# Running sums of the gates as rows of a product, and the last two heads' mask on TensorE, in a hybrid decoder block

## Chip, cores and metric

The kernel runs on one core of a Trainium2 chip. The metric is the time of the whole program on the device, in microseconds, taken as the median of several runs; smaller is better. A core has five engines with queues of their own, worked off in order: TensorE (PE in the profile, its weight loads PEld), VectorE (DVE), ScalarE (ACT), GpSimd (POOL) and SyncE (SP, which here only starts DMAs). Matrix products are written to the accumulator memory PSUM; all other tiles lie in the on-chip memory SBUF, and larger intermediate arrays in device memory.

## The reference

A decoder block over 1024 tokens of width 1024: forgetting attention (8 heads of 64) and a chunked spatial gate side by side, an output projection, then a gated MLP with a causal depthwise convolution. The change concerns the attention:

```
xn = rmsnorm(h, norm_mix_g); proj = xn @ w_in
log_f = log_sigmoid(proj[..., G_END:] + b_forget)          # one gate per head and token
c = cumsum(log_f, axis=1)
logits = einsum('bqhd,bkhd->bhqk', q, k) * Dh ** -0.5
logits = logits + c_q - c_k                                # running sums of query and key
logits = where(causal, logits, -inf)
p = softmax(logits); out = einsum('bhqk,bkhd->bqhd', p, v)
mix = concat([out, spatial_gate], -1); h = h + mix @ w_out
```

In a softmax over the keys the query's own sum `c_q` cancels, so the kernel needs only the key's `c_k`.

## The kernel before

**Precision.** Operands of the large products are split into a high part, rounded to the type in which TensorE takes them, and a low part, the rest; a product is made of high x high, high x low and low x high.

**Stages.** Queries, keys, gates and values are projected first. Queries and keys go to device memory as `qd` and `kd` (head, high or low, 64, 1024), through stores on SP's queue (L534). `forget` and `forget_sums` make the gates' running sums; `turn` transposes them to rows of 64 x 128, negates them and stores them as `ncd` (8 x 1024), from the middle of the first query and key step. Behind the attention come the output projection (L1026 to L1028) and the gated MLP (L1117, L1369).

**Attention.** `head_loads(h)` brings a head's operands: `ab[:, 0]` holds the query's high and low part on 64 partitions each, `ab[:, 1]` the key's likewise, `b2s` the key's parts in swapped order, and `cks` the row of `ncd` repeated on all 128 partitions. The head's two small tiles alternate between even and odd heads. `logits(h, j)` makes the logits of query block j (128 rows) for its (j+1) x 128 keys: in pieces of up to 512 columns two products, `A x B` (high x high plus low x low) and `A x B2` (high x low plus low x high), into one of two buffers of two PSUM banks (tag `L`). The signs are turned, so that masked entries are large and a minimum is sought. On POOL, `affine_select` sets the entries above the diagonal of the block's own 128 columns of `cks` to 3e38. Since a later (larger) block reads these columns unmasked, and blocks run from 7 down to 0, each select stands between two minima. On DVE one fused instruction adds logits and row, writes the result to SBUF and gives the row minimum; ACT takes the exponential of it in place with its sum.

`turn_p` transposes blocks of exponentials on PE, ACT copies the high part and DVE subtracts the low part (L813 to L815); `values` multiplies them with V (L832) and `row_tail` turns the reciprocal row sums (L738 to L742). `pair_half` scales and splits the outputs of two heads, for the first three pairs on POOL.

**Order.** PE's order in the attention is written out by hand: `seq` chains every PE instruction behind the one before. A step holds two groups of value products of head h, the transposes of the next step, and, by the table `NEXT`, up to two query blocks of logits of head h+1. Heads 6 and 7's logits are made in the steps of heads 5 and 6. Sixteen pieces of filler (`sg_out`, L874 to L876, twelve products each: the projection of the spatial gate) are spread over the steps up to head 4's by `FILLS`; their weights come in two halves, and the second half's low parts are made on DVE (called from L880). On the other engines a scheduler decides the order when the program is built, by program order and readiness; `after` adds an order without a wait. The lists `sels` hold the selects, and behind them `pair_half` and `wo_load` (splitting the output weights) are ordered on POOL, one instruction behind each select.

Of the kernel before, what the change touches and what calls it, by code (L numbers as in the profile page):

```python
# [14 lines left out]
P = 128  # L15
# [50 lines left out]
def block_kernel(ctx: ExitStack, tc: tile.TileContext, xT, xtok, wuv, wv, wqk, wf, cpk, bfv,  # L66
# [73 lines left out]
    qd = drm.tile([8, 2, 64, 1024], F32, name="qd")  # L140
    kd = drm.tile([8, 2, 64, 1024], F32, name="kd")
    rbd = drm.tile([8, P], F32, name="rbd")
    ncd = drm.tile([8, 1024], F32, name="ncd")
    vd = drm.tile([2, P, 2, 512], F32, name="vd")
    hpd = drm.tile([8, P, 1024], F32, name="hpd")
    h2d = drm.tile([8, P, 1024], F32, name="h2d")
# [309 lines left out]
    def forget():  # L456

        c = sb("gg", [P, 512])
        r = sb("gg", [P, 512], F32R)
        wfa, sel = c[:, 0:128].rearrange("p (a b) -> p a b", b=8), c[0:64, 128:136]  # L460
        bfb, z, e, rows = c[:, 136:144], c[:, 144:208], c[:, 208:272], c[0:64, 272:400]
        tri, ones, lh, ll = r[:, 0:P], r[:, P:2 * P], r[:, 256:320], r[:, 320:384]
        sp.dma_start(out=wfa[:, 0:8, :], in_=wf)
        sp.dma_start(out=bfb, in_=bfv.to_broadcast((P, 8)))
        dve.tensor_tensor(out=wfa[:, 8:12, :], in0=wfa[:, 0:4, :], in1=wfa[:, 4:8, :], op=ALU.add)
        dve.tensor_scalar(out=wfa[:, 12:16, :], in0=wfa[:, 0:4, :], scalar1=-1.0, scalar2=None, op0=ALU.mult)
        dve.tensor_tensor(out=sel, in0=ident[0:64, 0:8], in1=ident[0:64, 32:40], op=ALU.add)

        one128 = one[:, 0:1].to_broadcast((P, P))
        act.copy(ones, one128)  # L470
        dve.scalar_tensor_tensor(out=tri, in0=maskb, scalar=0.0, in1=ident, op0=ALU.is_gt, op1=ALU.add)
        w = sb(RTAG[rn[0] % 6], [P, 16, 64], F32R)
        rn[0] += 1
        dve.memset(f32(w), 0.0)
        dve.tensor_copy(w[:, :, 0:8], wfa)
        dve.tensor_tensor(out=w[:, :, 32:40], in0=wfa, in1=f32(w[:, :, 0:8]), op=ALU.subtract)
        zr = sb(RTAG[rn[0] % 6], [64, 1024])
        rn[0] += 1
        for hf in range(2):
            ps = sbank()  # L480
            ops = ([("B11", k, k) for k in range(4)] + [("B21", k, 4 + k) for k in range(4)] if hf == 0 else
                   [("B22", k, 8 + k) for k in range(4)] + [("T3", k, 12 + k) for k in range(4)])
            for i, (n, k, wi) in enumerate(ops):
                for s in range(2):
                    pe.matmul(ps[0:64, :], w[:, wi, :], xs(n, s, k), start=(i == 0 and s == 0),
                              stop=(i == 7 and s == 1))
            act.copy(zr[:, hf * 512:hf * 512 + 512], ps[0:64, :])
        return c, r, zr

    def forget_sums(c, r, zr):  # L490
        sel, bfb, z, e, rows = c[0:64, 128:136], c[:, 136:144], c[:, 144:208], c[:, 208:272], c[0:64, 272:400]
        tri, ones, lh, ll = r[:, 0:P], r[:, P:2 * P], r[:, 256:320], r[:, 320:384]
        v3 = lambda t: t.rearrange("p (h t) -> p h t", h=8)
        ps = sbank()
        for tt in range(8):
            pe.matmul(ps[:, tt * 8:(tt + 1) * 8], zr[:, tt * P:(tt + 1) * P], sel, start=True, stop=True)
        dve.tensor_tensor(out=v3(z), in0=ps[:, 0:64].rearrange("p (t h) -> p h t", h=8),
                          in1=rstd1.unsqueeze(1).to_broadcast((P, 8, 8)), op=ALU.mult)
        dve.tensor_tensor(out=v3(z), in0=v3(z), in1=bfb.unsqueeze(2).to_broadcast((P, 8, 8)), op=ALU.add)
        dve.scalar_tensor_tensor(out=e, in0=z, scalar=-1.0, in1=z, op0=ALU.mult, op1=ALU.max)  # L500
        act.activation(e, e, AF.Exp, scale=-1.0)
        act.activation(e, e, AF.Ln, bias=one[:, 0:1])
        dve.tensor_scalar(out=z, in0=z, scalar1=-1.0, scalar2=0.0, op0=ALU.mult, op1=ALU.max)
        dve.tensor_tensor(out=z, in0=z, in1=e, op=ALU.add)
        dve.tensor_copy(lh, z)
        dve.tensor_tensor(out=ll, in0=z, in1=f32(lh), op=ALU.subtract)

        for o, m in ((64, tri), (128, ones)):
            pe.matmul(ps[:, o:o + 64], m, lh, start=True, stop=False)
            pe.matmul(ps[:, o:o + 64], m, ll, start=False, stop=True)  # L510
        whole, run = v3(ps[:, 128:192]), v3(e)
        dve.memset(run[:, :, 0:1], 0.0)
        for tt in range(1, 8):
            dve.tensor_tensor(out=run[:, :, tt:tt + 1], in0=run[:, :, tt - 1:tt], in1=whole[:, :, tt - 1:tt], op=ALU.add)
        dve.tensor_tensor(out=v3(z), in0=v3(ps[:, 64:128]), in1=run, op=ALU.add)

        def turn():
            pe.transpose(ps[0:64, 192:320], z, ident)
            act.activation(rows, ps[0:64, 192:320], AF.Copy, scale=-1.0)
            sp.dma_start(out=ncd.rearrange("h (t p) -> (h t) p", p=P), in_=rows)  # L520

        return turn

# [204 lines left out]
    loads = [None] * 8  # L728
    exs = []
    rows = [None] * 8  # L730
    sels = [[] for _ in range(8)]

    def row_tail(h):

        p, hh, rs = h // 2, h % 2, rows[h]
        ptr = bank()
        rt = sb("t01", [8, P])
        dve.reciprocal(rs, rs)  # L738
        seq(pe.transpose(ptr[0:8, 0:P], rs, ident))
        act.copy(rt, ptr[0:8, 0:P])  # L740
        act.dma_start(out=rsd[h], in_=rt)
        sp.dma_start(out=attF[p][hh * 64:hh * 64 + 64, 1, :],  # L742
                     in_=rsd[h].rearrange("a b -> (a b)").unsqueeze(0).to_broadcast((64, 1024)))

    def pair_half(p, o):

        if attT[p] is None:
            attT[p] = sb("A" if p < 2 else "G", [P, 2, 1024], F32R)
        f, t = attF[p], attT[p]
        if p < 3:  # L750
            s = sels[2 * p + 3][o.start // 512 * 3:]
            after(tc, pool.tensor_tensor(out=f[:, 0, o], in0=f[:, 0, o], in1=f[:, 1, o], op=ALU.mult), s[0])
            after(tc, pool.tensor_copy(t[:, 0, o], f[:, 0, o]), s[1])
            after(tc, pool.tensor_tensor(out=t[:, 1, o], in0=f[:, 0, o], in1=f32(t[:, 0, o]), op=ALU.subtract), s[2])
# [6 lines left out]
    psa.release()  # L761
    psa = tc.alloc_tile_pool(name="psb", bufs=4, space=bass.MemoryType.PSUM, reuse_waits="tile")

    cks, b2s = sb("x2", [P, 2, 1024]), sb("x2", [P, 2, 1024], F32R)
    abs_, places = [None] * 8, {}

    def head_loads(h):
# [1 line left out]
        abs_[h] = ab  # L769
        hh = h % 2  # L770
        sp.dma_start(out=f32(ab[:, 0, :]), in_=qd[h].rearrange("s d t -> (s d) t"))
        sp.dma_start(out=f32(ab[:, 1, :]), in_=kd[h].rearrange("s d t -> (s d) t"))
        sp.dma_start(out=cks[:, hh, :], in_=ncd[h:h + 1, :].to_broadcast((P, 1024)))
        sp.dma_start(out=f32(b2s[0:64, hh, :]), in_=kd[h, 1])
        loads[h] = sp.dma_start(out=f32(b2s[64:128, hh, :]), in_=kd[h, 0])
        rows[h] = sml.tile([P, 8], F32, tag="rs", name=nm("rs"))

    def logits(h, j):


        i, jj, hh = j // 2, j % 2, h % 2
        A, B, ck, B2 = abs_[h][:, 0, :], abs_[h][:, 1, :], cks[:, hh, :], b2s[:, hh, :]
        w1, w2 = (2 * i + 1) * P, (2 * i + 2) * P
        if jj == 1:
            tp = sb(TTAG[i][hh], [P, w1 + w2])
# [1 line left out]
        t = places[h, i][jj]  # L787
        n = (j + 1) * P
        qs = slice(j * P, (j + 1) * P)
        sels[h].append(pool.affine_select(out=ck[:, qs], in_=ck[:, qs], pattern=[[-1, P]], compare_op=ALU.is_ge,  # L790
                                          fill=BIG, base=0, channel_multiplier=1))
        mn = sml.tile([P, 1], F32, tag="mn", name=nm("mn"))
        ps = psa.tile([P, 1024], F32, tag="L", bufs=2, name=nm("pl"))
        for c in range(0, n, 512):
            e = min(n, c + 512)
            seq(pe.matmul(ps[:, c:e], A[:, qs], B[:, c:e], start=True, stop=False))  # L796
            seq(pe.matmul(ps[:, c:e], A[:, qs], B2[:, c:e], start=False, stop=True))  # L797
        dve.tensor_tensor_reduce(out=t, in0=ps[:, 0:n], in1=ck[:, 0:n], scale=1.0, scalar=lim[:, 0:1],  # L798
                                 op0=ALU.add, op1=ALU.min, accum_out=mn)
        exs.append(act.activation(t, t, AF.Exp, bias=mn, scale=-1.0, accum_out=rows[h][:, j:j + 1]))  # L800

# [43 lines left out]
    def sg_out():  # L845
# [17 lines left out]
        for hf in range(2):  # L863
            o = slice(hf * 512, hf * 512 + 512)
            for tt in range(8):
# [11 lines left out]
                dve.tensor_tensor(out=hs, in0=ps, in1=hs, op=ALU.add)  # L877
                sp.dma_start(out=hpd[tt, :, o], in_=hs)
                if hf == 0 and tt == 7:
                    whs = split(nxt, "dve")  # L880
                yield

    filler = sg_out()
# [3 lines left out]
    def wo_load(ks):  # L887
        for k in ks:
# [6 lines left out]
                w = [t[:, :, hf * 512:hf * 512 + 512] for hf in range(2)]  # L895
            for hf in range(2):
                src = wr[:, hf * 512:hf * 512 + 512]
                s = sels[6][4 * k + 2 * hf:] if k < 2 else sels[7][7:] * 2
                after(tc, pool.tensor_copy(w[hf][:, 0], src), s[0])
                after(tc, pool.tensor_tensor(out=w[hf][:, 1], in0=src, in1=f32(w[hf][:, 0]), op=ALU.subtract), s[1])  # L900
            wo.append(w)

    STEPS = [[(h, i, 2 * c) for i in (3, 2, 1, 0) for c in range(i + 1)] for h in range(8)]
# [612 lines left out]
```

## Time and profile before

| | |
|---|---|
| time, median of 3 runs | 1076.82 us (1076.59 to 1077.02) |
| the profiled execution | 1076.44 us, its span 1074.7 us |
| granted TensorE clock | 0.998 |
| PE busy | 1054.8 us, 98% of the span |
| DVE, ACT, POOL busy | 892.9, 571.0, 237.2 us |
| attention | about 222 to 387 us of the span |

A row of a view names the line of the kernel, the engine, the operation, the tile written and those read (buffer numbers left out), the shape and the count, then the busy time, the mean of one in ns, the idle time of the engine just before such instructions and what ended it. In a view by time a row begins with the start and the duration in microseconds. A wait is written as waiting engine and tile, arrow, the engine and tile that ended it, then total, count and longest wait. PE's matmuls overlap in their pipeline: one of 512 columns shows 389 ns, yet the next starts 227 ns later, so that short gaps between starts don't show as idle time.

### The profile page before, as it was taken

What the parts mean: (1) busy time and instruction counts of PE and PEld (TensorE: products, weight loads), DVE (VectorE), ACT (ScalarE), POOL (GpSimd) and SP (SyncE); (2) the same over time, 40 slices, a digit from 0 to 9 for tenths busy, and PEclk for the clock granted to TensorE, in tenths of its full rate; (3) what the DMA queues carried; (4) which work ended last, traced back from release to release, by engine and by line L of the source; (5) the groups of instructions that cost most, each with busy time, mean ns of one, the idle gap of its engine ahead of it and who ended that gap; (6) DMA issues with size and microseconds to landing.
All of it is one profiled execution on the core that took longest, in us unless ns stands there. A gap on an engine that the chain in (4) does not pass through costs nothing.

```text
span 1074.7 us, 14461 instructions
## 1 busy us (share of the span) xinstructions
PE 1054.8 (98%) x5013; PEld 875.8 (81%) x5013; DVE 892.9 (83%) x1303; ACT 571.0 (53%) x985; POOL 237.2 (22%) x219
## 2 busy tenths in 40 slices
PE   9999999989999899999999999999999999999997
PEld 6888788778888788878888888888888888888886
DVE  5985798777777869999899999989988776898774
ACT  6666644456666845764444444444444444454653
POOL 0002134020223651054333333333322000000000
PEclk9999999999999999999999999999999999999999
DMA  9242257957556335132244523223331899433442
GB/s 338 97 140 97 68 159 213 265 165 215 162 177 225 120 128 185 72 118 97 98 137 161 172 69 127 99 98 99 107 118 46 289 327 319 123 95 97 140 125 96
DMA packets 66297, 160.80 MB, mean 150 GB/s; under 512 B 7976, under 2 KB 8240, under 8 KB 66224
## 3 DMA queue, kind: packets, MB, share of 16 engines
q1 hardware_dynamic: 65792, 159.32, 45.5%
q8 instruction: 39, 0.64, 0.2%
q10 hardware_dynamic: 432, 0.57, 0.1%
q14 instruction: 34, 0.28, 0.1%
HBM read 117.06 MB, written 42.80 MB: 149 GB/s over the span
## 4 chain that ended last, share of the span: by engine, by line
PE 74%; DVE 2%; issue 2%; DMA 2%; ACT 2%; POOL 0%; DVEq 0%; ACTq 0%; POOLq 0%; SPq 0%
PE k L1369 19%; PE qa L1117 11%; PE qc L1117 11%; PE qd L1117 11%; PE qb L1117 5%; PE pb L832 2%; PE pb L813 2%; PE pf L874 1%; PE pf L876 1%; PE pf L875 1%; PE pl L796 1%; PE pl L797 1%; DMA raw<-wos 1%; PE pb L1026 1%; PE pb L1028 1%
## 5 line engine op out<-in xcount | busy, mean ns | idle before, releaser
L1369 PE MATMUL k<-whb,wha 128*128 128x512 f32 x924 | 209.7, 389 | 0.0
L1369 PEld LDWEIGHTS k<-whb,wha 128*128 128x128 f32 x924 | 173.3, 188 | 36.2 <-DVE wha L160 0.2
L1117 PE MATMUL qc<-xT,whb 128*128 128x512 f32 x540 | 129.8, 389 | 0.0
L1117 PE MATMUL qa<-xB,wha 128*128 128x512 f32 x528 | 127.2, 390 | 0.0
L1117 PEld LDWEIGHTS qc<-xT,whb 128*128 128x128 f32 x540 | 101.3, 188 | 21.2 <-ACT whb L154 0.2
L1117 PEld LDWEIGHTS qa<-xB,wha 128*128 128x128 f32 x528 | 98.8, 188 | 20.8 <-DVE wha L160 0.4
L154 ACT CAST wha<-sg 128x512 fp32r<-128x512 f32 x77 | 47.7, 622 | 96.9 <-PE k L1369 86.6
L154 ACT CAST whb<-sg 128x512 fp32r<-128x512 f32 x82 | 50.6, 618 | 85.8 <-PE qc L1117 68.5
L160 DVE TENSOR_TENSOR wha<-sg,wha 128x512 fp32r<-128x512 f32 x77 | 52.8, 688 | 41.0 <-ACT wha L154 40.9
L1117 PE MATMUL qd<-xB,whb 128*128 128x512 f32 x264 | 63.8, 389 | 0.5 <-DVE h L1236 0.5
L1117 PE MATMUL qd<-xT,whb 128*128 128x512 f32 x264 | 63.6, 389 | 0.0
L815 DVE TENSOR_TENSOR pt<-pb,pt 128x512 fp32r<-128x512 f32 (+1 forms) x80 | 50.0, 635 | 14.5 <-ACT pt L814 13.4
L160 DVE TENSOR_TENSOR whb<-sg,whb 128x512 fp32r<-128x512 f32 x82 | 58.3, 711 | 4.4 <-ACT whb L154 4.3
L1117 PE MATMUL qb<-xT,whb 128*128 128x512 f32 x252 | 60.8, 389 | 0.0
L1004 POOL TENSOR_TENSOR sg<-raw 128x512 f32<-128x512 f32 x20 | 30.9, 1546 | 134.2 <-DVE whb L160 76.0
L1117 PEld LDWEIGHTS qd<-xB,whb 128*128 128x128 f32 x264 | 49.5, 188 | 11.2 <-issue 0.9
L1117 PEld LDWEIGHTS qd<-xT,whb 128*128 128x128 f32 x264 | 49.5, 188 | 10.3
L1117 PEld LDWEIGHTS qb<-xT,whb 128*128 128x128 f32 x252 | 47.3, 188 | 9.8
L814 ACT CAST pt<-pb 128x512 fp32r<-128x512 f32 (+1 forms) x80 | 42.5, 539 | 20.6 <-PE pb L813 14.7
L832 PE MATMUL pb<-pt,V 128*128 128x256 f32 x320 | 51.4, 285 | 1.3 <-DVE pt L815 1.2
L790 POOL TENSOR_SCALAR_AFFINE_SELECT x<-x 128x128 f32<-128x128 f32 x64 | 19.9, 312 | 129.7 <-DVE mn L798 77.4
L1007 POOL TENSOR_TENSOR sg<-sg,raw 128x512 f32<-128x512 f32 x20 | 33.3, 1664 | 64.1 <-DVE whb L160 64.1
(396 smaller groups left out, 2305.7 us busy)
## 6 DMA issues: line engine op xcount, KB each, us to landing
raw<-wup SPq DMA_DIRECT2D x44, 512.0 KB, 3.7
sg<-hx SPq DMA_DIRECT2D x77, 256.0 KB, 2.6
hx<-hs SPq DMA_DIRECT2D x44, 256.0 KB, 3.8
hx<-ca SPq DMA_DIRECT2D x35, 256.0 KB, 2.0
xT<-wdn SPq DMA_DIRECT2D x28, 256.0 KB, 4.3
raw<-wqk SPq DMA_DIRECT2D x8, 512.0 KB, 3.6
qd<-G SPq DMA_DIRECT2D x16, 256.0 KB, 3.5
kd<-G SPq DMA_DIRECT2D x16, 256.0 KB, 3.3
```

Of the source, the lines that this page charges most:

```text
L154: act.copy(h, src)
L160: return eng.tensor_tensor(out=l, in0=src, in1=f32(h), op=ALU.subtract)
L790: sels[h].append(pool.affine_select(out=ck[:, qs], in_=ck[:, qs], pattern=[[-1, P]], compare_op=ALU.is_ge, fill=BIG, base=0, channel_multi ...
L796: seq(pe.matmul(ps[:, c:e], A[:, qs], B[:, c:e], start=True, stop=False))
L813: seq(pe.transpose(ptr[:, c:c + P], tj[jj][:, k * P:(k + 1) * P], ident))
L814: act.copy(pt[:, 0, 0:w], ptr[:, 0:w])
L815: dve.tensor_tensor(out=pt[:, 1, 0:w], in0=ptr[:, 0:w], in1=f32(pt[:, 0, 0:w]), op=ALU.subtract)
L832: seq(pe.matmul(po[0][:, oo:oo + n], lhs, pt[:, s, o:o + n], start=(k == 0 and s == 0), stop=(s == 1 and half)))
L1004: pool.tensor_tensor(out=s[0], in0=a21, in1=a22, op=ALU.add)
L1007: pool.tensor_tensor(out=s[3], in0=s[1], in1=a12, op=ALU.add)
L1117: pe.matmul(ps, w[:, wi, ks], xb[:, xi, k, :], start=(first and n == 0), stop=(n == 11), skip_group_check=True)
L1369: pe.matmul(banks[bk + m], xh[:, xi, ms], wh[:, wi, :], start=(first and p_ == 0 and n == 0), stop=(p_ == NP - 1 and n == 2), skip_group_c ...
```

## The change

It does four things. The negated running sums are split into a high and a low part and stored as two rows per head; the logits' second product takes them in: its key side is the key's low part (64 rows) and these two rows, its query side the query's high part and two rows of ones (`oned`), 66 rows in all. Its first product now takes the key's high part twice, so high x high plus low x high; the low x low term is left out. With that the broadcast row and the selects go. For heads 0 to 5 the fused minimum adds a constant mask instead (`msk`, 896 columns of zeros and a block of 3e38 above the diagonal, one bf16 tile for all heads, of which the last n columns are read). For heads 6 and 7 the mask of the diagonal block is a product of its own (identity times mask block in bf16), a plain reduction takes the minimum from PSUM, and ACT reads the exponential's input straight from PSUM. Beside that, `pair_half` and `wo_load` run on POOL without the order behind selects, the second filler weights' low parts move from DVE to POOL, and the small tiles of `row_tail` share one buffer with the mask.

```diff
-    ncd = drm.tile([8, 1024], F32, name="ncd")
+    ncd = drm.tile([2, 8, 1024], F32, name="ncd")
+    oned = drm.tile([2, 1024], F32, name="oned")
...
         act.copy(ones, one128)
+        sp.dma_start(out=oned.rearrange("s (t p) -> (s t) p", p=P), in_=f32(ones[0:16, :]))
...
             pe.transpose(ps[0:64, 192:320], z, ident)
-            act.activation(rows, ps[0:64, 192:320], AF.Copy, scale=-1.0)
-            sp.dma_start(out=ncd.rearrange("h (t p) -> (h t) p", p=P), in_=rows)
+            rh, rl = r[0:64, 0:P], r[0:64, P:2 * P]
+            act.activation(rh, ps[0:64, 192:320], AF.Copy, scale=-1.0)
+            dve.scalar_tensor_tensor(out=rl, in0=ps[0:64, 192:320], scalar=-1.0, in1=f32(rh),
+                                     op0=ALU.mult, op1=ALU.subtract)
+            for s, t in enumerate((rh, rl)):
+                sp.dma_start(out=ncd[s].rearrange("h (t p) -> (h t) p", p=P), in_=f32(t))
...
-    sels = [[] for _ in range(8)]
+    idr = sb("t01", [P, 1024])
+    idb = idr[:, 512:576].bitcast(BF16)
+    pool.tensor_copy(idb, ident)
+    msk = idr[:, 0:512].bitcast(BF16)
+    pool.memset(msk[:, 0:1024 - P], 0.0)
+    pool.tensor_copy(msk[:, 1024 - P:1024], maskb)
...
-        rt = sb("t01", [8, P])
+        rt = idr[0:8, 640 + P * hh:640 + P * (hh + 1)]
...
-            s = sels[2 * p + 3][o.start // 512 * 3:]
-            after(tc, pool.tensor_tensor(out=f[:, 0, o], in0=f[:, 0, o], in1=f[:, 1, o], op=ALU.mult), s[0])
...
+            pool.tensor_tensor(out=f[:, 0, o], in0=f[:, 0, o], in1=f[:, 1, o], op=ALU.mult)
...
-    cks, b2s = sb("x2", [P, 2, 1024]), sb("x2", [P, 2, 1024], F32R)
+    a2s, b2s = sb("x2", [P, 2, 1024], F32R), sb("x2", [P, 2, 1024], F32R)
...
         sp.dma_start(out=f32(ab[:, 0, :]), in_=qd[h].rearrange("s d t -> (s d) t"))
-        sp.dma_start(out=f32(ab[:, 1, :]), in_=kd[h].rearrange("s d t -> (s d) t"))
-        sp.dma_start(out=cks[:, hh, :], in_=ncd[h:h + 1, :].to_broadcast((P, 1024)))
-        sp.dma_start(out=f32(b2s[0:64, hh, :]), in_=kd[h, 1])
-        loads[h] = sp.dma_start(out=f32(b2s[64:128, hh, :]), in_=kd[h, 0])
+        for s in range(2):
+            sp.dma_start(out=f32(ab[s * 64:s * 64 + 64, 1, :]), in_=kd[h, 0])
+        sp.dma_start(out=f32(a2s[0:64, hh, :]), in_=qd[h, 0])
+        if h < 2:
+            sp.dma_start(out=f32(a2s[64:66, hh, :]), in_=oned)
+        sp.dma_start(out=f32(b2s[64:66, hh, :]), in_=ncd[:, h, :])
+        loads[h] = sp.dma_start(out=f32(b2s[0:64, hh, :]), in_=kd[h, 1])
...
-        A, B, ck, B2 = abs_[h][:, 0, :], abs_[h][:, 1, :], cks[:, hh, :], b2s[:, hh, :]
+        A, B, A2, B2 = abs_[h][:, 0, :], abs_[h][:, 1, :], a2s[0:66, hh, :], b2s[0:66, hh, :]
...
-        sels[h].append(pool.affine_select(out=ck[:, qs], in_=ck[:, qs], pattern=[[-1, P]], compare_op=ALU.is_ge,
-                                          fill=BIG, base=0, channel_multiplier=1))
...
             seq(pe.matmul(ps[:, c:e], A[:, qs], B[:, c:e], start=True, stop=False))
-            seq(pe.matmul(ps[:, c:e], A[:, qs], B2[:, c:e], start=False, stop=True))
-        dve.tensor_tensor_reduce(out=t, in0=ps[:, 0:n], in1=ck[:, 0:n], scale=1.0, scalar=lim[:, 0:1],
+            if h > 5 and e == n:
+                seq(pe.matmul(ps[:, n - P:n], idb, maskb, start=False, stop=False, skip_group_check=True))
+            seq(pe.matmul(ps[:, c:e], A2[:, qs], B2[:, c:e], start=False, stop=True))
+        if h > 5:
+            dve.tensor_reduce(out=mn, in_=ps[:, 0:n], axis=AX.X, op=ALU.min)
+            exs.append(act.activation(t, ps[:, 0:n], AF.Exp, bias=mn, scale=-1.0, accum_out=rows[h][:, j:j + 1]))
+            return
+        dve.tensor_tensor_reduce(out=t, in0=ps[:, 0:n], in1=msk[:, 1024 - n:1024], scale=1.0, scalar=lim[:, 0:1],
                                  op0=ALU.add, op1=ALU.min, accum_out=mn)
...
-                    whs = split(nxt, "dve")
+                    whs = split(nxt, "pool")
...
-                s = sels[6][4 * k + 2 * hf:] if k < 2 else sels[7][7:] * 2
-                after(tc, pool.tensor_copy(w[hf][:, 0], src), s[0])
+                pool.tensor_copy(w[hf][:, 0], src)
...
```

More of the change, by code (lines that the diff above doesn't have):

```diff
@@ L460, in forget @@
         wfa, sel = c[:, 0:128].rearrange("p (a b) -> p a b", b=8), c[0:64, 128:136]
-        bfb, z, e, rows = c[:, 136:144], c[:, 144:208], c[:, 208:272], c[0:64, 272:400]
-        tri, ones, lh, ll = r[:, 0:P], r[:, P:2 * P], r[:, 256:320], r[:, 320:384]
+        bfb = c[:, 136:144]
+        tri, ones = r[:, 0:P], r[:, P:2 * P]
         sp.dma_start(out=wfa[:, 0:8, :], in_=wf)
@@ L490, in forget_sums @@
     def forget_sums(c, r, zr):
-        sel, bfb, z, e, rows = c[0:64, 128:136], c[:, 136:144], c[:, 144:208], c[:, 208:272], c[0:64, 272:400]
+        sel, bfb, z, e = c[0:64, 128:136], c[:, 136:144], c[:, 144:208], c[:, 208:272]
         tri, ones, lh, ll = r[:, 0:P], r[:, P:2 * P], r[:, 256:320], r[:, 320:384]
@@ L750, in pair_half @@
         if p < 3:
-            s = sels[2 * p + 3][o.start // 512 * 3:]
-            after(tc, pool.tensor_tensor(out=f[:, 0, o], in0=f[:, 0, o], in1=f[:, 1, o], op=ALU.mult), s[0])
-            after(tc, pool.tensor_copy(t[:, 0, o], f[:, 0, o]), s[1])
-            after(tc, pool.tensor_tensor(out=t[:, 1, o], in0=f[:, 0, o], in1=f32(t[:, 0, o]), op=ALU.subtract), s[2])
+            pool.tensor_tensor(out=f[:, 0, o], in0=f[:, 0, o], in1=f[:, 1, o], op=ALU.mult)
+            pool.tensor_copy(t[:, 0, o], f[:, 0, o])
+            pool.tensor_tensor(out=t[:, 1, o], in0=f[:, 0, o], in1=f32(t[:, 0, o]), op=ALU.subtract)
         else:
@@ L897, in wo_load @@
                 src = wr[:, hf * 512:hf * 512 + 512]
-                s = sels[6][4 * k + 2 * hf:] if k < 2 else sels[7][7:] * 2
-                after(tc, pool.tensor_copy(w[hf][:, 0], src), s[0])
-                after(tc, pool.tensor_tensor(out=w[hf][:, 1], in0=src, in1=f32(w[hf][:, 0]), op=ALU.subtract), s[1])
+                pool.tensor_copy(w[hf][:, 0], src)
+                pool.tensor_tensor(out=w[hf][:, 1], in0=src, in1=f32(w[hf][:, 0]), op=ALU.subtract)
             wo.append(w)
```

## The prediction

> **What bounds the kernel now.** I first read busy time by stage, cutting the span where the attention stage begins and ends, where its filler products run out, and where its last logits are done.
>
> ```profile
> 222.00:346.00 124.00, 120.59 (x755) 105.38 (x756) 92.99 (x191) 82.51 (x178) 31.75 (x64) 1.00 0.59 181
> 346.00:380.00 34.00, 29.63 (x220) 26.91 (x219) 28.82 (x61) 26.83 (x62) 19.31 (x31) 1.00 0.38 125
> 380.00:387.00 7.00, 6.33 (x53) 6.13 (x54) 4.44 (x9) 5.35 (x11) 5.04 (x6) 1.00 0.36 117
> 387.00:858.00 471.00, 470.47 (x2106) 389.02 (x2106) 423.64 (x496) 225.69 (x331) 143.93 (x88) 1.00 0.36 124
> ```
>
> After each length come the busy times of PE, its weight loads, DVE, ACT and POOL. Behind 387 us PE is idle for 0.5 us in 471, so a microsecond saved before 387 is saved at the end. In front of it PE is idle for 3.4, 4.4 and 0.7 us, together 8.5: no relief of the other engines can bring more. The granted clock is 1.00 throughout. Next, who ended PE's waits, in the first and in the second of these stretches:
>
> ```profile
> PE pb L813 <- DVE pt L815: 1.5, 4, 0.7
> PE pl L796 <- DVE mn L798: 1.2, 2, 0.7
> PE pb L832 <- DVE pt L815: 0.2, 1, 0.2
> ```
> ```profile
> PE pb L739 <- DVE rs L738: 1.5, 1, 1.5
> PE pb L813 <- DVE pt L815: 1.4, 2, 0.7
> PE pb L832 <- DVE pt L815: 1.0, 2, 0.6
> ```
>
> All of them name DVE. The second stretch is the one with heads 6 and 7's logits and nearly no filler; there DVE is busy 28.8 and ACT 26.8 of 34 us. That is where the change can pay.
>
> **The change part by part.**
>
> *Selects on POOL go.* Sixty-four diagonal selects leave POOL. A select could start only when the minimum before it had read the row, and the next minimum waited for it. DVE's groups up to 346 us, with the idle time before them:
>
> ```profile
> L798 DVE CUSTOM_DVE_ANT_0 t<-pl,x,lim 128x1024 f32<-128x1024 f32 (+3 forms) x12 | 12.9, 1078 | 1.5 <-POOL x L790 0.8 <-PE pl L797 0.7
> L798 DVE CUSTOM_DVE_ANT_0 H<-pl,x,lim 128x1024 f32<-128x1024 f32 (+3 forms) x12 | 12.9, 1077 | 2.1 <-POOL x L790 1.2 <-PE pl L797 0.9
> L798 DVE CUSTOM_DVE_ANT_0 gg<-pl,x,lim 128x256 f32<-128x256 f32 (+1 forms) x12 | 4.9, 406 | 0.8 <-POOL x L790 0.8
> L160 DVE TENSOR_TENSOR whl<-raw,whl 128x512 fp32r<-128x512 f32 x4 | 2.7, 707 | 0.0
> ```
>
> POOL cost DVE 0.8 + 1.2 + 0.8 = 2.8 us. Most of it lies under PE's filler products: PE's own waits for a minimum are 1.2 us. Between 0 and 2.8 I take half of PE's waits, -0.6.
>
> *Four subtractions of the second filler weights move from DVE to POOL*, the 2.7 us of the last row. They stand in front of two subtractions of attention blocks:
>
> ```profile
> 283.20 0.55 PE L813 MATMUL pb<-ident,t 128*128 128x128 f32 x3 [0.68 <-DVE pt L815]
> ```
> ```profile
> 285.78 0.40 PE L874 MATMUL pf<-whl,G 128*128 128x512 f32 x1
> ```
> ```profile
> 281.51 1.07 ACT L814 CAST pt<-pb 128x512 fp32r<-128x512 f32 x2
> ```
> ```profile
> L160 POOL TENSOR_TENSOR whl<-raw,whl 128x512 fp32r<-128x512 f32 x4 | 5.0, 1284 | 3.8 <-ACT whl L154 3.8
> ```
>
> The last row is cut from the view of POOL; four pieces take POOL 5.1 us. I take the 0.7 us wait, -0.7 (0 to -1.5, all such waits of the stretch). The weights must be there for the product at 285.8: from ACT's casts, just ahead of 281.5, POOL has the time for it, since its selects are gone; if it is held up, PE's filler waits by as much.
>
> *Loads.* Each head loads 1.54 MB, not 2.05 (the broadcast row and one half less), but four of its transfers now fill 64 partitions instead of two.
>
> ```profile
> 204.00:206.00 2.00, 2.00 (x10) 1.66 (x9) 1.06 (x3) 0.76 (x2) 0.00 (x0) 1.00 1.01 414
> 206.00:211.00 5.00, 5.00 (x23) 4.13 (x22) 2.64 (x3) 1.52 (x2) 1.02 (x1) 1.00 1.04 229
> ```
>
> The last two columns are the DMA share and GB/s: with full queues, 414 before the half-height loads are reached and 229 after. So a head's loads cost 1.5/0.414 + 0.5/0.229 = 5.8 us before and 0.5/0.414 + 1.0/0.229 = 5.6 after: next to nothing gained. [...] By bytes alone the filler weights behind the loads would land 2.5 us earlier and the first logits lose their wait (0.7 at most); I take -0.2.
>
> *Heads 6 and 7.* DVE's minimum no longer writes, and its result is read without a further instruction. The stretch from 346 us:
>
> ```profile
> L798 DVE CUSTOM_DVE_ANT_0 t<-pl,x,lim 128x1024 f32<-128x1024 f32 (+3 forms) x4 | 4.3, 1080 | 0.7 <-PE pl L797 0.4 <-POOL x L790 0.3
> L798 DVE CUSTOM_DVE_ANT_0 gg<-pl,x,lim 128x256 f32<-128x256 f32 (+1 forms) x4 | 1.6, 409 | 0.0
> L798 DVE DVE_READ_ACCUMULATOR2_ANT mn<- 128x1 f32 x16 | 1.3, 82 | 0.0
> ```
> ```profile
> L44 DVE TENSOR_REDUCE gms<-pt 128x16 f32<-128x1024 f32 x4 | 4.8, 1216 | 0.7 <-ACT pt L44 0.7
> ```
>
> The first two rows average 832 and 192 columns, so the fused form costs 1.05 ns a column and 207 ns; the only plain reduction, 1024 columns in 1216 ns, then has 141 ns beside the columns. Each logits tile saves 66 + 82 = 148 ns, sixteen 2.4 us of DVE's 28.8. With the select wait (0.3) DVE has 2.7 us less to do where PE idles 4.4 waiting for it. ACT keeps its exponentials, so I count 2.0 of it (0 to -2.7).
>
> *Mask products.* Sixteen bf16 products of 128 columns are new on PE; eight transposes of that width show what a weight load and 128 columns cost:
>
> ```profile
> 246.55 1.00 PE pb L813 x8
> ```
>
> 0.125 us each, 2.0 us in all, where PE has 4.4 idle: +0.4 taken, by the share of PE's time there that nothing covers (0 to +2.0; they can only add, and +3.7 if a change of type cost the 0.23 us of the array rival below).
>
> *Two logits buffers, held longer.* In heads 6 and 7 a buffer comes free after the exponential, not after the minimum. ACT's exponentials of head 6, and PE's products that would now need their buffers:
>
> ```profile
> 355.38 0.94 ACT L800 ACTIVATE t<-t,mn 128x768 f32<-128x768 f32 x1 [0.81 <-DVE mn L798]
> 356.78 0.83 ACT L800 ACTIVATE t<-t,mn 128x640 f32<-128x640 f32 x1
> 360.08 0.62 ACT L800 ACTIVATE wy<-wy,mn 128x384 f32<-128x384 f32 x1
> ```
> ```profile
> 356.01 0.46 PE L796 MATMUL pl<-x 128*128 128x512 f32 x1
> 357.01 0.34 PE L796 MATMUL pl<-x 128*128 128x384 f32 x1
> 360.38 0.28 PE L796 MATMUL pl<-x 128*128 128x128 f32 x1
> ```
>
> The exponentials end 0.3, 0.6 and 0.3 us after PE gets there: 1.2 us for a head, 2.4 for two. PE's queue is in order, so transposes and value products behind these logits wait too; but just there PE goes on to wait for DVE anyway. I take +0.4 (0 to +2.4).
>
> *Products with 66 rows.* Columns and count stay, so I take 0; the other end is a rival below. *The sums' two rows* add a subtraction on DVE and a second store, and the ones a store that waits for ACT's copy:
>
> ```profile
> 138.20 1.12 SPq L520 DMA_DIRECT2D ncd<-gg  x1
> ...
> 142.00 1.22 SPq L534 DMA_DIRECT2D qd<-G  x2
> ```
> ```profile
> 116.15 0.28 ACT L44 CAST gg<-one 128x128 fp32r<-128x128 f32 x1
> ```
> ```profile
> L402 PE MATMUL qa<-V,whl x36: 389/389/389, 131.0 to 172.0; 128*128 128x512 f32 x36
> ```
>
> Between SP's two stores lie 2.7 us of slack. The weights queued behind the ones' store are first used at 131.0, 15 us behind the copy that it waits for; should SP hold them longer, PE would wait one for one. I take 0.
>
> Sum: -0.6 -0.7 -0.2 -2.0 +0.4 +0.4 = -2.7. The profiled execution took 1076.44 us (its span 1074.7 and 1.74 around it), which gives 1073.7; the median is 0.38 above that execution, so I predict **1074.1**.
>
> **The rivals.**
>
> *Hidden anyway.* In the crowded stretch ACT, which keeps all its work, sets the pace as soon as DVE is relieved; the new products and the buffer stalls eat the rest. For it: ACT's 26.8 of 34. Against it: every wait of PE names DVE. Then the crowded stretch brings 0 in place of -1.2, and 1.5 is left: 1075.3; with half of the other gains hidden too, 1076.1. I call it 1075.7.
>
> *The buffers decide (slower).* Each of heads 6 and 7's tiles goes product, minimum, exponential before its buffer returns, and ACT does exponentials in line with its copies. If PE arrives first, as in the three pairs above, the stall of 2.4 us delays the transposes, hence ACT's copies, hence the next exponential; DVE's relief (2.0) is then waited away and the mask products' 2.0 stand in the path. 2.4 + 2.0 - 1.5 = +2.9: 1079.7. It decides from the point where the stalls outlast the idle time that follows them on PE. For it: ACT's 26.8; against it: that idle time of 4.4 us.
>
> *Sixty-six rows switch the array (slower).* The one place where operands of 64 rows alternate with full ones, and the pace of full ones:
>
> ```profile
> 118.22 1.66 PE L402 MATMUL qb<-H,whl 128*128 128x512 f32 x6
> 119.81 1.05 PE L496 MATMUL ps<-gg,whl 64*128 64x8 f32 x8
> ```
> ```profile
> 477.27 2.72 PE qa L1117 x12
> ```
>
> Six full products take 1.59 us to the next start, not 1.36: 0.23 us are lost at the turns. Attention has 12 such pairs a head, 96 in all: 22 us, at most 4 of it in idle time, less the gains: 1076.8 + 22 - 4 - 1.5 = 1093. [...]
>
> *More than forecast.* Each in-order queue is laid out anew without the selects; if all 4.4 us of the crowded stretch close and 2 of the 3.4 before it, the time is 1076.8 - 6.4 = 1070.4.
>
> **How the numbers follow.** Forecast 0.46, more than forecast 0.10, hidden 0.24, buffers 0.15, sixty-six rows 0.05. About 0.2% (2.15 us) can be told from no change: below 1074.7 is faster. The first two and a little of the third make 0.57; the rest of the third and a little of the first and fourth 0.25; slower 0.18. From 1070.0 to 1079.2 the range holds all but the worst of the buffers and the 66 rows; the forecast's own range is 1072.5 to 1075.
>
> **What would show it.** Right: minima of heads 6 and 7 at about 1.2 us for 1024 columns, PE's idle time from 346 to 380 us shrunk by one to two, no wait for weights near 285. Wrong: starts between full and 66-row products more than 0.23 us apart (the array), PE waiting for exponentials (the buffers), PE's waits unchanged but now ended by ACT (hidden).

## The result, and the profile after

| | before | after |
|---|---|---|
| time, median of 4 runs | 1076.92 us (1076.59 to 1077.91) | 1087.23 us (1086.09 to 1087.86) |
| ratio to before, 95% interval | | 1.0095 (1.008 to 1.011) |
| profiled execution, its span | 1076.44, 1074.7 us | 1087.22, 1085.5 us |
| TensorE's first logits of head 0 start at | 223.43 | 224.32 |
| head 0's row sums are turned at | 246.28 | 252.60 |
| head 5's row sums are turned at | 349.18 | 356.60 |
| output projection starts at | 387.08 | 397.06 |

The change made the kernel 10.3 us slower, where 2.7 us less was forecast. The four starts divide the 10.8 us by which the span grew: 0.9 before the attention, 5.4 between the first logits and head 0's sums, 1.1 in the next five heads, 2.6 from there to the output projection, 0.8 behind it.

Who ended TensorE's waits in the attention, after (the same view as in the prediction, from 222 to 400 us; its first six of twelve rows):

```profile
PE pf L895 <- ACT whl L155: 2.4, 1, 2.4
PE pf L895 <- DVE pt L836: 2.1, 2, 1.1
PE pb L752 <- DVE rs L751: 2.0, 2, 1.3
PE pb L712 <- DVE V L44: 1.9, 1, 1.9
PE pb L834 <- DVE pt L836: 1.5, 2, 1.1
PE pf L896 <- POOL whl L161: 0.8, 1, 0.8
```

The first, the second and the sixth row are new: before, no filler product (`pf`) waited. In the first and the sixth the filler waits for the fourth piece of its first weights, whose cast on ScalarE and subtraction on GpSimd come late; the second is taken up below. Here are ScalarE and then TensorE by time (start, duration, idle time before in brackets):

```profile
225.18 1.67 ACT L155 CAST whl<-raw 128x512 fp32r<-128x512 f32 x3
...
228.71 1.15 ACT L821 ACTIVATE t<-t,mn 128x1024 f32<-128x1024 f32 x1
...
230.88 1.53 ACT L714 CAST G<-pb 128x512 fp32r<-128x512 f32 x3
232.30 0.95 ACT L821 ACTIVATE t<-t,mn 128x768 f32<-128x768 f32 x1
...
233.23 0.61 ACT L155 CAST whl<-raw 128x512 fp32r<-128x512 f32 x1
```
```profile
231.11 0.39 PE L897 MATMUL pf<-whl,G 128*128 128x512 f32 x1
233.90 0.50 PE L895 MATMUL pf<-whl,G 128*128 128x512 f32 x1 [2.40 <-ACT whl L155]
235.25 0.50 PE L896 MATMUL pf<-whl,G 128*128 128x512 f32 x1 [0.84 <-POOL whl L161]
...
237.88 0.63 PE L895 MATMUL pf<-whl,G 128*128 128x512 f32 x1
238.31 0.63 PE L896 MATMUL pf<-whl,G 128*128 128x512 f32 x1
```

Three casts of the weights run at 225, the fourth at 233: copies of the turned gate, the load of the exponential's table and the exponentials of 1024, 896 and 768 columns stand between them in ScalarE's queue. In the kernel before all four had run ahead of any of these:

```profile
220.94 2.40 ACT L154 CAST whl<-raw 128x512 fp32r<-128x512 f32 x4 [5.88 <-DMA raw<-wos]
```

The stall costs twice. It takes 2.57 us between the two starts at 231.11 and 233.90 beyond a product's usual pace, and 1.12 more behind 233.90; then products of 512 columns start 0.43 us apart (237.88, 238.31), not 0.23: the granted clock is down. Windows of the changed kernel (length; busy PE, PEld, DVE, ACT, POOL; granted clock; DMA share; GB/s):

```profile
236.00:240.00 4.00, 4.00 (x13) 3.19 (x13) 2.34 (x5) 1.70 (x4) 0.00 (x0) 0.59 0.36 131
240.00:246.00 6.00, 5.26 (x27) 4.29 (x26) 2.19 (x8) 1.59 (x6) 0.00 (x0) 1.00 0.56 180
```

The slow products lie between about 235.9 and 239.3 us, where the granted clock was 0.50 (from 236 to 239 us); ahead of them stand two waits of 2.4 and 0.8 us with a product between them. At about half the pace these 3.4 us lose half of their length, 1.7 (an estimate from the 0.43 and 0.23 us between starts); with 2.57 and 1.12 that makes up the 5.4 us lost here.

The later losses look alike but smaller. ScalarE at the step in which head 2's logits are made, after and before:

```profile
281.02 0.94 ACT L821 ACTIVATE t<-t,mn 128x768 f32<-128x768 f32 x1 [1.69 <-DVE mn L819]
...
281.95 0.81 ACT L821 ACTIVATE t<-t,mn 128x640 f32<-128x640 f32 x1
...
282.77 0.84 ACT L835 CAST pt<-pb 128x384 fp32r<-128x384 f32 x2
```
```profile
275.72 0.46 ACT L814 CAST pt<-pb 128x384 fp32r<-128x384 f32 x1
276.08 0.83 ACT L800 ACTIVATE t<-t,mn 128x640 f32<-128x640 f32 x1
...
276.90 0.46 ACT L814 CAST pt<-pb 128x384 fp32r<-128x384 f32 x1
```

Before, a copy that frees a bank for TensorE ran between the exponentials of 768 and 640 columns; after, both copies wait for both. The second row of the first view, TensorE's two waits of 1.1 us for `pt`, is these places (heads 2 and 4), and in head 6's logits the exponential of 1024 columns has likewise moved ahead of a copy.

### The profile page after: what moved, and what is told of

Read it like the earlier page. It is cut to its first block, busy times and chain, and to the rows that moved or that the text cites. A ratio compares the mean times of both kernels' runs of the same rounds, so it can differ in the third digit from the quotient of the medians.

```text
span 1085.5 us, 14318 instructions
## 1 busy us (share of the span) xinstructions
PE 1060.5 (98%) x5029; PEld 878.3 (81%) x5029; DVE 891.0 (82%) x1284; ACT 570.3 (53%) x985; POOL 222.0 (20%) x162
## 4 chain that ended last, share of the span: by engine, by line
PE 74%; DVE 6%; ACT 4%; issue 2%; DMA 1%; POOL 0%; SPq 0%; DVEq 0%; ACTq 0%; POOLq 0%
PE k L1389 19%; PE qa L1137 11%; PE qc L1137 11%; PE qd L1137 11%; PE qb L1137 5%; PE pb L853 2%; PE pb L834 2%; PE ps L259 2%; DVE G L44 1%; PE pf L895 1%; PE pf L896 1%; PE pf L897 1%; PE pl L810 1%; PE pl L813 1%; PE pb L1046 1%
## 5 line engine op out<-in xcount | busy, mean ns | idle before, releaser
L1137 PEld LDWEIGHTS qd<-xT,whb 128*128 128x128 f32 x264 | 49.5, 188 | 10.3
L853 PEld LDWEIGHTS pb<-pt,V 128*128 128x128 f32 x320 | 44.3, 190 | 2.9 <-issue 1.3
```

What stands on the lines that cost most here:

```text
L853: seq(pe.matmul(po[0][:, oo:oo + n], lhs, pt[:, s, o:o + n], start=(k == 0 and s == 0), stop=(s == 1 and half)))
L1137: pe.matmul(ps, w[:, wi, ks], xb[:, xi, k, :], start=(first and n == 0), stop=(n == 11), skip_group_check=True)
```

## Theories

**A**: the loss is the order in which ScalarE's queue was laid out when the changed kernel was built; exponentials now stand ahead of casts and copies that TensorE needs sooner. **B**: more loads stand ahead of the filler's weights on SP, so the weights land later. **C**: the new form of heads 6 and 7 costs (mask products, buffers held through the exponential). **D**: the second filler weights' subtractions come too late on GpSimd.

## Experiments

**One place in the queue.** `b1_cast_late` puts only the late cast into the kernel before; `e1_casts_first` takes it out of the changed kernel.

```
-  split_w(wr, (w[:, 0], w[:, 1]), "act", lo_eng)
+  act.copy(w[:, 0], wr) if len(whs) < 3 or len(exs) > 3 else after(tc, act.copy(w[:, 0], wr), exs[2]); ...
```


> The kernel before, with one order added: the fourth cast of the filler's first weights on ScalarE stands behind head 0's exponential of 768 columns, where the changed kernel has it. No product, load or mask is changed. Theory A: the first filler waits for it and the time rises by about 5.4, to 1082.3, with a stretch of lower clock behind the wait as in the changed kernel. Theory B: the loads are those of before, so the time stays at 1076.9. A middle value would say that the place of the cast costs only the wait itself (some 3.5 us) and that the rest belongs to something else.

Measured: 1083.87 us (1082.45 to 1084.84), ratio 1.0062 (1.0049 to 1.0076). Three of the four rows of TensorE's waits from 222 to 246 us, and two windows:

```profile
PE pf L874 <- ACT whl L858: 3.1, 1, 3.1
PE pb L705 <- DVE V L44: 1.9, 1, 1.9
PE pf L875 <- POOL whl L858: 0.9, 1, 0.9
```
```profile
224.00:227.00 3.00, 3.00 (x12) 2.50 (x11) 2.25 (x4) 0.88 (x2) 0.99 (x1) 0.64 0.25 87
...
236.00:240.00 4.00, 4.00 (x12) 3.25 (x13) 2.08 (x4) 0.87 (x2) 0.29 (x1) 0.57 0.38 131
```

One cast in another place makes the kernel before 6.9 us slower, with the changed kernel's picture: wait, then low clock. B cannot explain that, since the loads are those of before. For part of the 1.5 us over the forecast the profile has a mark of its own: in this execution the clock was also low from 224 to 227 us, behind the 1.9 us wait for `V` that the kernels before and after have too. Its two executions with the highest granted clock, 0.997, took 1082.45 and 1083.24 us, near the 1082.3 forecast.

```
-  whs = split(load(0), "pool")
+  whs = split(load(0), "pool"); yield
...
-  turn_sg(0)
+  turn_sg(0); next(filler)
```


> The changed kernel, with the split of the filler's first weights called ahead of head 0's logits, so that ScalarE's queue has all four casts of them in front of the first exponential; nothing is computed differently. Theory A (the loss is the place of the fourth cast in ScalarE's queue, behind the exponentials of 768 and more columns): no wait of TensorE for whl of ScalarE is left in the first filler, head 0's row sums are turned 5.4 us earlier (near 247.2 instead of 252.60), and the time falls by about 5.4 to near 1081.8. Theory B (the weights land later, because more loads stand ahead of them on SP): the casts now wait for the landing and the time stays near 1087.2. Theory C (the loss lies in heads 6 and 7): near 1087.2 too.

Measured: 1086.08 us (1085.82 to 1086.45), ratio 1.0085 (1.0071 to 1.0099): 1.1 us gained, not 5.4. The wait for `whl` is gone, but TensorE stands in the same place:

```profile
232.20 0.54 PE L895 MATMUL pf<-whl,G 128*128 128x512 f32 x1 [3.49 <-DVE G L715]
```

The filler's first product needs a PSUM bank that the turned gate's second half holds, and its copies still stood behind the exponentials of 1024 and 896 columns. So A in its narrow form (that one cast) does not explain the changed kernel by itself; what is left is that two things which the filler needs had both gone behind the exponentials.

**The whole order ahead of the filler.** `e4_prologue_order` fixes by hand the order of casts, copies and exponentials on ScalarE, and of head 0's minima behind the gate's subtractions on VectorE.

```
+  sgc.append(act.copy(sgT[c][:, 0, o], ps)); after(tc, sgc[-1], casts[3])
+  sgd.append(dve.tensor_tensor(out=sgT[c][:, 1, o], ...))
...
+  mi = dve.tensor_tensor_reduce(...); h or after(tc, mi, sgd[3])
...
+  casts.append(act.copy(w[:, 0], wr)); ...
...
+  next(filler); turn_sg(0)
...
+  turn_sg(1); after(tc, exs[0], sgc[5]); after(tc, exs[1], exs[0])
```


> The changed kernel with ScalarE's and VectorE's order ahead of the first filler made what it was in the kernel before: the four casts of the filler's first weights, then the copies of the turned gate's first half, then those of its second half, and only then the exponentials of 1024 and 896 columns. (Casting early alone left a wait of 3.5 us in the same place, for the bank that the second half's copy frees.) Theory A, widened (the loss ahead of head 0 is ScalarE's order, whichever of the filler's two needs stands behind the exponentials): no wait of TensorE over 1 us between 228 and 240 us but the usual ones, no stretch of lower clock there, row sums of head 0 turned near 247.2 instead of 252.60, and the time near 1081.8. Theory A': the first minimum and exponential come later by this, and a wait of some 3 us takes the old one's place: 1085 to 1087.

Measured: 1081.95 us (1081.41 to 1083.75), ratio 1.0053 (1.0041 to 1.0066); head 0's sums are turned at 247.16. Both as A had it (1081.8, 247.2). Its casts tell of B too:

```profile
220.22 2.41 ACT L879 CAST whl<-raw 128x512 fp32r<-128x512 f32 x4 [4.35 <-DMA raw<-wos]
```

The weights are there at 220.2, 0.7 us earlier than before the change (220.94). They do not land later; B falls as a delay in time.

**What turned the order round.** `e8_wos_first` adds no order. It only issues the two loads of the filler's weights ahead of both heads' first loads.

```
-  whs = split(load(0), "pool")
+  w0_ = load(0); yield; whs = split(w0_, "pool")
...
-  head_loads(0)
+  next(filler); head_loads(0)
```


> The changed kernel with the two loads of the filler's first weights issued ahead of both heads' first loads on SP (in the changed kernel four more loads stand ahead of them than before); no order is added by hand, and the build then puts the four casts ahead of the gate's copies and of the exponentials, as in the kernel before. If the number of loads ahead of these weights is what turned ScalarE's order round: no wait of TensorE for whl or for the bank of the gate's copies, and the time falls by the same 5.2 that the order made by hand was worth, to near 1082.0. If the heads' loads, now later by two, become the wait instead: TensorE stands before its first logits, and 1084 or more.

Measured: 1081.12 us (1080.15 to 1081.58), ratio 1.0038 (1.0024 to 1.0052). ScalarE has the fourth cast ahead of the gate's copies again, and two of the second half's copies ahead of the exponentials:

```profile
215.74 0.61 ACT L155 CAST whl<-raw 128x512 fp32r<-128x512 f32 x1
...
226.70 1.07 ACT L714 CAST G<-pb 128x512 fp32r<-128x512 f32 x2 [1.51 <-PE pb L712]
...
229.09 1.15 ACT L821 ACTIVATE t<-t,mn 128x1024 f32<-128x1024 f32 x1
```

The waits for `whl` and for the bank are gone as in `e4_prologue_order`. So B is right in another sense than it was meant: where the weights' loads stand among the others decides where their casts come to stand in ScalarE's queue when the program is built, though on the chip the weights are not late. How the build weighs the loads is not shown.

**The copies in the heads' steps.** `e5_copies_first` leaves the prologue alone.

```
+  ptc.append(act.copy(pt[:, 0, 0:w], ptr[:, 0:w]))
...
+  now, turned = ...; h < 7 and s in (1, 3) and after(tc, exs[-1], ptc[-2])
```


> The changed kernel, whose prologue is left alone, with one order added in each head's steps: the last exponential of a step stands behind the first copy of the next turn, as the kernel before had it for the exponential of 640 columns. Theory A: the waits of 1.2 us behind the logits of heads 2 and 4 and those in head 6's logits go; the stretch from head 0's turned sums to the output projection, 144.46 us against 140.80 before, loses 0.9 + 0.9 + 1.6, and the time falls by 3.4 to near 1083.8. Theory C (the new form of heads 6 and 7 itself, its mask products and its longer hold of the logits' buffers): only the 1.8 of heads 2 and 4, near 1085.4. The order is no matter: 1087.2.

Measured: 1083.64 us (1083.59 to 1084.68), ratio 1.0066 (1.0053 to 1.0079): 3.6 us gained, A's number (1083.8). ScalarE at head 2's logits, now in the order of before:

```profile
281.93 0.46 ACT L835 CAST pt<-pb 128x384 fp32r<-128x384 f32 x1
282.29 0.83 ACT L821 ACTIVATE t<-t,mn 128x640 f32<-128x640 f32 x1
```

From head 0's to head 5's sums it takes 102.28 us (after 104.00, before 102.90), from there to the output projection 38.42 (40.46; 37.90): the second gain, 2.0 us, lies where C had seen the form of heads 6 and 7. The edit goes a little beyond the order of before: it also puts the exponentials of 1024 columns of heads 1, 3, 5 and 7 behind a copy that they preceded in the kernel before.

**Both orders.** `e6_both_orders` joins the two edits.

> Both orders in one kernel. Theory A: the two gains add up, 5.4 and 3.4, near 1078.4; with what the change itself was forecast to save (2.7) still to be seen in the stretches between, so not below 1074. Theory C: near 1080.

Measured: 1077.85 us (1076.83 to 1079.18), ratio 1.0009 (1.0000 to 1.0018). The gains add up (5.3 and 3.6 alone, 9.4 together), and 9.4 of the 10.3 us lost are back by order alone. The kernel before was not run with the same orders, so this does not yet say what the change itself is worth.

**Heads 6 and 7 as the others.** `e2_heads_alike` on the changed kernel, `e7_both_alike` with both orders: `h > 5` becomes `h > 7` in both places, so that mask products and exponentials from PSUM go.

> The changed kernel with heads 6 and 7 treated as the others: mask added in VectorE's reduction, no mask product on TensorE, exponential from SBUF. Theory C (the new form of heads 6 and 7 costs what the stretch from head 4's turned sums to the output projection has lost, 59.88 us against 57.31): 2.6 us faster, near 1084.6. Theory A: these heads lose by the order that the build gives their queues, which this edit changes too, so nothing sure, within 1 us of 1087.2. As the prediction had it (the new form saves 2.0): near 1089.2.

Measured: 1086.29 us (1083.98 to 1087.17), ratio 1.0081 (1.0068 to 1.0094): by the median alone inconclusive. In its profile the stretch from head 5's sums to the output projection shrank from 40.46 to 38.12 us, but a lower clock about the first logits (0.66 from 222 to 227 us) and a longer one behind the filler's wait (0.74 from 240 to 246, where the changed kernel has 1.00) used up the gain. Its two executions at the changed kernel's granted clock, 0.997, took 1083.98 and 1084.63 us, which is C's number; only the next run tells form from order.

> Both orders, and heads 6 and 7 treated as the others (mask added in VectorE's reduction, exponential from SBUF, no mask product). Theory A (heads 6 and 7 lose by order alone): as with both orders and the new form, 1078.4, within 1 us. Theory C (the form itself costs): 1 to 2 us less than that kernel. As the prediction had it (the form saves 2.0): 2 us more.

Measured: 1077.02 us (1076.37 to 1078.06), ratio 1.0003 (0.9994 to 1.0012). With the orders right the old form is ahead by 0.8 us in the medians, their intervals overlap, and the stretch takes 38.10 against 38.40 us. So of C's 2.3 us 0.3 are left in the stretch, the rest was the order's; the saving of 2.0 that was forecast is not there either. Who ended TensorE's waits from about 346 us to the end of head 7, in `e6_both_orders` and in `e7_both_alike`:

```profile
PE pb L752 <- DVE rs L751: 2.0, 2, 1.3
PE pb L834 <- ACT t L753: 0.8, 1, 0.8
```
```profile
PE pb L752 <- DVE rs L751: 2.6, 2, 1.5
PE pb L834 <- DVE pt L836: 1.1, 2, 0.5
PE pb L853 <- DVE pt L836: 1.0, 2, 0.6
```

The new form has 2.8 us of such waits, the old 4.7: 1.9 saved. What eats them is mostly the mask products. One piece of 384 columns with its mask in the changed kernel, and without in `e2_heads_alike`:

```profile
358.52 0.34 PE L810 MATMUL pl<-x 128*128 128x384 f32 x1
358.70 0.23 PE L812 MATMUL pl<-maskb,t 128*128 128x128 bf16 x1
358.74 0.42 PE L813 MATMUL pl<-x,x 66*128 66x384 f32 x1
359.00 0.58 PE L853 MATMUL pb<-pt,V 128*128 128x256 f32 x4
```
```profile
361.07 0.34 PE L810 MATMUL pl<-x 128*128 128x384 f32 x1
361.25 0.34 PE L813 MATMUL pl<-x,x 66*128 66x384 f32 x1
361.43 0.57 PE L853 MATMUL pb<-pt,V 128*128 128x256 f32 x4
```

From the first product to the one behind the piece it is 0.48 us with the mask and 0.36 without, 0.12 more. Read so for all sixteen blocks of heads 6 and 7, the pieces sum to 7.4 us in `e6_both_orders` and 5.3 in `e7_both_alike`: 2.1 for the masks, 0.13 each. And 0.8 of the waits left, those for `t`, stand behind a table load on ScalarE:

```profile
380.48 1.28 ACT L966 ACT_TABLE_LOAD   x1
```

**The moved subtractions.** `e3_dve_again` is the changed kernel with `split(nxt, "dve")`.

> The changed kernel with the four subtractions of the filler's second weights on VectorE again, as before. As the prediction had it: 0.7 slower, near 1087.9. Theory D (on GpSimd they come too late for the filler): faster by up to 1 us, near 1086.2. Theory A: TensorE waits for neither, so within 0.5 us of 1087.2.

Measured: 1089.54 us (1089.21 to 1090.89), ratio 1.0119 (1.0105 to 1.0133): 2.3 us slower than the changed kernel. D falls; GpSimd was in time. VectorE and then TensorE in this kernel:

```profile
289.75 1.77 DVE L161 TENSOR_TENSOR whl<-raw,whl 128x512 fp32r<-128x512 f32 x2
291.44 1.27 DVE L836 TENSOR_TENSOR pt<-pb,pt 128x512 fp32r<-128x512 f32 x2
```
```profile
292.17 0.55 PE L834 MATMUL pb<-ident,t 128*128 128x128 f32 x3 [1.63 <-DVE pt L836]
```

The subtractions again hold up an attention block. From head 0's to head 5's sums it is 105.46 us against 104.00: 1.5 is the move's. Another 0.9 lies ahead of the attention, where a wait of TensorE for a gate tile was 1.6 us in this profile and 0.7 in that of the changed kernel. It was 1.6 in `e6_both_orders` and 0.7 in `e7_both_alike` too, which have the same code there (first logits at 225.24 and 223.60 us), so it can differ without any edit. Whether all of the 2.3 us between the medians is the move's is therefore not shown.

**A version that beats both?** Two moves that do not belong to the change, on `e6_both_orders`, on `e7_both_alike` and on the kernel before: heads 6 and 7's row sums turned behind the next transposes, and ScalarE's table load for the square root behind the last pair's copies.

```
+  tails.append(act.copy(t[:, 0, o], f[:, 0, o]))
...
-  row_tail(h)
+  h < 6 and row_tail(h)
...
-  for g, pt, js in zip(step, now, NEXT[s]):
+  for g, pt, js in zip(step, now, NEXT[s]) if (s, h) not in ((1, 6), (1, 7)) or row_tail(h) is None else ():
...
-  after(tc, act.activation(pad[:, 0:1], eps, AF.Sqrt), exs[-1])
+  after(tc, act.activation(pad[:, 0:1], eps, AF.Sqrt), tails[-1])
```


> The kernel with both orders (1077.85), with two further moves that have nothing to do with the change: the turning of the row sums of heads 6 and 7 stands behind the next step's turns instead of ahead of them, and ScalarE's table load for the square root stands behind the last pair's copies. Its profile showed TensorE waiting 1.46 and 0.89 us for these sums and 0.92 us for a bank behind the table load. All three go: 3.2 less, near 1074.6. Only the first two: near 1075.5. The late sums of head 7 hold up the last pair instead: 1077 to 1078.

> The same two moves on the kernel with both orders and heads 6 and 7 as the others (1077.02), whose profile showed 1.66 and 1.27 us of waits for the sums and none behind the table load: 2.9 less, near 1074.1. Theory C (the form of heads 6 and 7 costs): at or below the kernel with the new form. If the new form is worth what its shorter minimum saves: that one is the faster by 1 or more.

> The kernel before with the same two moves, and nothing of the change: its profile showed waits of 1.68 and 1.27 us for the sums, so 2.9 less than 1076.9, near 1074.0. Beside it the two kernels with the moves say what the change is worth once the orders are alike: the prediction had 2.7 less than this (near 1071.3); theory A, with the sums of the stretches so far, has no difference, within 1 us.

Measured: 1076.24 us (1074.95 to 1077.63), ratio 0.9996 (0.9987 to 1.0005); 1076.37 (1075.20 to 1077.98), 0.9997 (0.9989 to 1.0006); and 1085.74 (1084.65 to 1088.90), 1.0088 (1.0074 to 1.0102). The first two gained 1.6 and 0.7 us where 3.2 and 2.9 were expected, and neither can be told from the kernel before. In their profiles the stretch from head 5's sums to the output projection is 36.26 and 36.83 us: with the table load out of the way the new form is 0.6 ahead there, too little to show in the medians. The third, meant as the control, became 8.8 us slower than the kernel before where 2.9 less was expected: its profile has a new wait of 7.0 us at the first output product, and TensorE's clock is down behind it: products of 512 columns start 0.43 us apart from 393.55 us on, 0.23 in the kernel before, and the granted clock of the whole execution is 0.994.

```profile
392.98 0.77 PE L1026 MATMUL pb<-whl,A 128*128 128x512 f32 x1 [7.02 <-DVE H L841]
```
```profile
391.43 0.69 DVE L756 TENSOR_TENSOR H<-H 128x512 f32<-128x512 f32 x1 [5.24 <-DMA H<-rsd]
392.15 0.69 DVE L841 TENSOR_TENSOR H<-pb,H 64x512 f32<-64x512 f32 x1
```

VectorE waits 5.2 us for the broadcast row sums of head 7, and behind it stands the instruction that frees TensorE's bank. The kernel before has the same wait on VectorE, 4.2 us, but there TensorE took another bank first; that moving the turn shifted the banks' rotation is read from the code and was not tried. So what the change is worth on top of these two moves stays open.

## Why the prediction was wrong, step by step

**The step that failed** is *Loads*, -0.2. It weighed bytes and rates and asked when the weights land. That was right as far as it went: they land 0.7 us earlier, and this is hidden. (Its bytes are a little low, four full tiles of 128 x 1024 numbers of 4 bytes being 2.10 MB and three 1.57, but the two sums stay as near to each other.) But the prediction treated each engine's queue as given, except in one rival, and there ("Each in-order queue is laid out anew without the selects") the new layout could only gain. Being slower had a chance of 0.18, all of it for the buffers and the array, and neither of these came. More loads ahead of the weights moved the cast and the gate's copies behind the exponentials. That cost 5.3 us by the order made by hand and 6.1 by the loads' place alone (`e8_wos_first`). The second new layout, copies behind exponentials in the heads' steps, cost up to 3.6, and the term *Selects* had no price for it either. That the lost waits for selects brought it about is argued and not shown: without them, two minima run back to back and the second exponential is ready sooner; no run put the selects back.

Point by point, with the orders mended where it says so:

- *Selects* -0.6 and *subtractions* -0.7: from head 0's to head 5's sums 102.29 us with both orders against 102.90, so -0.6 of the forecast -1.3, and how much of it is the orders' own is not known. The direction of the subtractions' move was right; undone in the changed kernel it costs 1.5 in this stretch.
- *Heads 6 and 7* -2.0: 1.9 us of waits saved once the order is right. The minimum of 1024 columns was priced at 1.2 us and takes 1.23. ScalarE's exponential of 1024 columns takes 1.12 us from PSUM, 1.15 from SBUF: its work there did not grow.
- *Mask products* +0.4: priced right (0.125 us; measured 0.13) and mis-sized in the sum: 2.1, because the idle time that was to cover them is what the shorter minimum had taken away. Counting both against the same 4.4 us was the error; together the two are worth next to nothing (0.3 us lost, or 0.6 gained with the table load moved).
- *Two logits buffers* +0.4: TensorE waits 0.2 us for an exponential in the changed kernel, and not at all with both orders. "The buffers decide" did not happen, though its time (1079.7) came closer than the forecast.
- *Sixty-six rows* 0: right, nothing is lost at the turns. Full and 66-row products of 512 columns start 0.23 us apart (224.56 and 224.79 in `e1_casts_first`), where the turns to 64-row ones had cost 0.23 in the kernel before.
- *The sums' two rows* 0: from the turned sums to the first logits it is 87.58 us, not 87.01, and TensorE waits 0.5 us for a weight's subtraction in the changed kernel's profile and not at all in that of the kernel before. The stretch is 0.6 of the 0.9 us lost before the attention; why was not tried. The 0.8 behind the start of the output projection stays open too.

"Hidden anyway" is what is left once order is out of the account: with both orders the kernel stands at 1077.0 to 1077.9, beside 1077.0 before.

## What to carry to other kernels

Where a scheduler lays out in-order queues, removing or adding instructions and loads anywhere can reorder an engine that the edit does not touch. Price an edit by what comes out of the build: compare the instruction lists, and look for long instructions that have moved ahead of short ones on which TensorE waits. Pin such places by hand before judging the edit itself; and do not count one idle time as cover for two terms.

## What the hardware showed

Behind a stall of TensorE of 3.5 us (`e1_casts_first`) the clock was down (0.57 from 232 to 236 us): products of 512 columns start 0.43 us apart for 3.4 us. A shorter stall did it now and then: behind the wait of 1.9 us at 220 the clock from 224 to 227 us was 0.64 in `b1_cast_late` and 0.66 in `e2_heads_alike`, and 1.00 in nine other profiles (`before`, `after`, `b2_tails_late`, `e1_casts_first`, `e3_dve_again` to `e7_both_alike`). What decides it is not shown. The time of `b1_cast_late` and `e2_heads_alike` varies with the clock: the executions at 0.997 took 1082.45 and 1083.24 us (`b1_cast_late`) and 1083.98 and 1084.63 (`e2_heads_alike`), those at 0.994 to 0.996 from 1083.87 to 1084.84 and from 1086.29 to 1087.17.
